# Moving operands of two feed-forward stages placed at many different addresses modulo 256 bytes

## The chip, the cores and the metric

One core of one Trainium2 chip runs the kernel. The metric is device microseconds from one launch, lower is better; times are given as the median of several runs. A profile is one execution of the program taken by the hardware profiler; its times are counted from its first instruction to its last (the span).

## What is computed

One decoder layer for a sequence of 512 tokens with a model width of 1024, in float32. Two feed-forward blocks (FFN 1 and FFN 2, inner width 2816) stand around a mixer that has two attention branches. Only the FFNs are touched by the change:

```python
def swiglu_ffn(x, g, w_gate, w_up, w_down):
    h = rms_norm(x, g)
    return (jax.nn.silu(h @ w_gate) * (h @ w_up)) @ w_down

x = x + 0.5 * swiglu_ffn(x, ffn1_norm, ffn1_w_gate, ffn1_w_up, ffn1_w_down)
# RMS norm, one wide projection, forgetting attention (branch A),
# top-k sparse attention (branch B), gated merge, output projection
x = x + merged @ w_out
x = x + 0.5 * swiglu_ffn(x, ffn2_norm, ffn2_w_gate, ffn2_w_up, ffn2_w_down)
```

## The kernel before

**Precision.** TensorE is fed in fp32r. Every float32 operand is split into a high and a low part, and each product takes three matmuls: high by high, low moving by high weights, high moving by low weights (`mm3`, L129 to L132). A name that ends in `h` or `l` is the high or the low part. In `PE.matmul(out, a, b)` the first operand is the stationary one (the weights, loaded by a LDWEIGHTS of 128 columns ahead of each matmul) and the second is the moving one, which is streamed past it.

**Orientation.** In the FFNs the weights are stationary (`wh`, `wl`, three buffers each of 128x1024) and the activations move: their features lie on the 128 partitions and the 512 tokens along a partition.

**Stages of an FFN** (`ffn`, L182). The 22 blocks of 128 inner features are worked in three groups: blocks 0 to 7, 8 to 15, 16 to 21.

- Blocks 0 to 5 are done plainly: eight k-steps of `mm3` with 512 moving columns for the gate product (`pg`) and again for the up product (`pu`), with `xh`, `xl` moving.
- The other sixteen blocks are done in eight pairs of blocks (`pair_steps`, L307) by a scheme that needs seven half-size products in place of eight. `product` (L317) runs 24 matmuls of 256 moving columns each, so that a pair takes 7 x 24 = 168 of them, and the two FFNs 2 x 8 x 168 = 2688. What moves here are combinations of the normalized input, made once by `combine` (L235) on VectorE and ScalarE: `b1` (once a pair), `tb`, `ta`, `b2` (twice a pair), each a high and a low tile made by `parts_tile` (L219) in the pool `halves`. They write to the PSUM tiles `pA`, `pB`, `pC`.
- After each group, `run_down` (L396) multiplies by the down weights: `pd`, 512 moving columns, where the group's activations move. Two blocks share one tile. The tiles `a0h` to `a2l` (made in `act_tiles`, L190, one set for all three groups) hold the first six blocks of a group; the last two blocks of the first and the second group lie in stream buffers (`ax`). In the last step of FFN 2 the 512 columns are done as twice 256, so that 36 matmuls there have 256 columns.

Of the 1038 matmuls of `pd` with 512 columns, 846 have one of `a0h` to `a2l` moving and 192 have `ax`. The profile shows `a0h`, `a1h`, `a2h` as `ah` and the low ones as `al`.

**Places.** A tile's address along its partition is set by the pools: tiles stand one behind another, and all sizes around are such that nearly every one begins at 96 modulo 256 bytes. In the built program this holds for all weights of the FFNs (`wh`, `wl`, and each 128-column slice of them, since slices are 512 bytes apart), for `xh`, `xl`, `ax`, for `a0h` to `a2l`, and in the mixer for `mh`, `ml` (moving in `ps_out`) and for the weights `wh`, `wl` that move in `ps_t` against `xh`, `xl`. The exception is the pool `halves`: a tile of 8 floats named `pad` (L188) stands ahead of it, so that `b1`, `tb`, `ta`, `b2` begin at 128 modulo 256. Steps within a tile are 1024 or 2048 bytes, so that each matmul of a tile begins at the tile's place. Below, *place* means the first byte of the moving operand modulo 256.

**Order.** TensorE's order of work is written out by hand (steps in `ffn`, weights loaded and split up to three steps ahead); the scheduler orders the other engines. The low part of the activations of most blocks (L204, L205) is made with a DMA that adds onto the negated high part, issued from GpSimd's queue.

Of the kernel before, what the change touches and what calls it, by code (L numbers as in the profile page):

```python
# [11 lines left out]
F32 = mybir.dt.float32  # L12
F32R = mybir.dt.float32r
# [5 lines left out]
P = 128  # L19
T = 512  # L20
# [22 lines left out]

GROUPS = ((0, 8), (8, 16), (16, 22))
PLAIN = 6
HT = T // 2
HK = KD // 2

# [2 lines left out]
def tile_hybrid_layer(ctx: ExitStack, tc: tile.TileContext, a: dict):  # L51
# [14 lines left out]
    def tmp_tile(name):  # L66
        return tmp.tile([P, T], F32, tag="t", name=name)
# [28 lines left out]
    def stream(i, dtype, name):  # L96

        return xpool.tile([P, 2 * T], dtype, tag=f"X{i}", name=name)
# [83 lines left out]
    def ffn(n, nxt, parts=lambda d: [slice(0, T)]):  # L182
        wg, wu, wp, wd = (a[f"w_{nm}{n}"] for nm in ("gate", "up", "pair", "down"))
        gi = 0 if n == 1 else 2
        with tc.tile_pool(name=f"ffn{n}", bufs=1) as ap, tc.tile_pool(name=f"halves{n}", bufs=1) as hp:
            act = {}

            hp.tile([P, 8], F32, name="pad")  # L188

            def act_tiles(f):  # L190

                q, lo = f // 2, next(lo for lo, hi in GROUPS if lo <= f < hi)
                j = q - lo // 2
                if q not in act:
                    act[q] = ([ap.tile([P, 2 * T], F32R, tag=f"a{j}{i}", name=f"a{i}") for i in "hl"]
                              if j < 3 else [stream(6 + i, F32R, "ax") for i in range(2)])
                return [t[:, f % 2 * T:f % 2 * T + T] for t in act[q]]

            def split_act(f, u, late):

                h, l = act_tiles(f)
                S.copy(h, u)  # L202
                if late:
                    S.mul(l, h.bitcast(F32), -1.0)  # L204
                    G.dma_start(l, u, accum_op=OP.add)  # L205
                else:
                    V.tensor_sub(l, u, h.bitcast(F32))  # L207

            def activate(f, pg, pu, rb):
# [5 lines left out]
                V.tensor_mul(u, u, g)  # L215
                split_act(f, u, 1 < f < PLAIN)


            def parts_tile(nm, cols):  # L219
                return [hp.tile([P, HK * cols], F32R, tag=nm + i, name=nm + i)  # L220
                        .rearrange("p (k t) -> p k t", k=HK) for i in "hl"]

            ops = {}

            def operand(nm, cols=T):
                if nm not in ops:
                    ops[nm] = parts_tile(nm, cols)
                return ops[nm]

            def split_to(nm, k, src, cols=T):  # L230
                h, l = (t[:, k] for t in operand(nm, cols))
                S.copy(h, src)
                V.tensor_sub(l, src, h.bitcast(F32))

            def combine(k):  # L235
# [3 lines left out]
                for dst, d in ((lo, k), (hi, k + HK)):  # L239
                    V.scalar_tensor_tensor(dst, x[d], gains[:, gi, d:d + 1], rbs[0], op0=OP.mult, op1=OP.mult)  # L240
                split_to("b1", k, lo[:, :HT], HT)
                yield
                ta, tb = tmp_tile("ta"), tmp_tile("tb")
                V.tensor_sub(ta[:, :HT], lo[:, :HT], lo[:, HT:])
                V.scalar_tensor_tensor(tb[:, :HT], ta[:, :HT], -1.0, hi[:, HT:], op0=OP.mult, op1=OP.subtract)
                V.tensor_sub(ta[:, HT:], hi[:, HT:], lo[:, HT:])
                V.scalar_tensor_tensor(tb[:, HT:], tb[:, :HT], -1.0, hi[:, :HT], op0=OP.mult, op1=OP.subtract)
                split_to("tb", k, tb)
# [5 lines left out]
            def moving(nm, half):  # L254
                h, l = ops[nm]
                sl = slice(half * HT, half * HT + HT)
                return (h, l) if nm == "b1" else (h[:, :, sl], l[:, :, sl])
# [17 lines left out]
            def plain(src, f, run):  # L275
                raw = {}

                def split():
                    return [t[:, :f * P].rearrange("p (n m) -> p n m", n=f) for t in split_w(raw["a"][0], f * P)]
                return Step(raw, [("a", f, src)], split, run, "a")  # L280
# [3 lines left out]
            def run_gate(f):  # L284
                def run(w):
                    pg[0] = fm_product(w, "pg", mid if f == 1 and n == 2 else {})
                    if f == 1 and n == 2:
                        activate(0, *pair0, held[0])
                        rbs.append(held[0])
                return run  # L290

            def run_up(f):
                def run(w):
                    if f == 1 and n == 1:

                        pu = fm_product(w, "pu", mid, psum.tile([P, T], F32, tag="s", bufs=2, name="pu1"))
                        activate(0, *pair0, held[0])
                        rbs.append(held[0])
                    else:
                        pu = fm_product(w, "pu")  # L300
                    if f == 0:
                        pair0.extend((pg[0], pu))
                    else:
                        activate(f, pg[0], pu, rbs[0])
                return run

            def pair_steps(q, last):  # L307
# [78 lines left out]

                load = {z: (z, 0, wp[q - PLAIN // 2, i]) for i, z in enumerate("abcd")}
                return [Step(raw, [load["c"], load["d"], load["a"]], split_a, run_a),
# [7 lines left out]
            def run_down(d, lo, hi):  # L396
                def run(w):
                    order = [k for k in range(hi - lo - 2)] + [hi - lo - 1, hi - lo - 2]
                    end = hi == KF

                    for cols in parts(d) if end else [slice(0, T)]:
                        ps = acc_tile("pd")[:, cols]
                        for k in order:
                            h, l = act_tiles(lo + k)
                            mm3(ps, w[0][:, k], w[1][:, k], h[:, cols], l[:, cols], k == order[0], k == order[-1])
                        V.scalar_tensor_tensor(x[d][:, cols], ps, 0.5, x[d][:, cols], op0=OP.mult, op1=OP.add)  # L406
                        if end:
                            nxt(d, cols)
                return run
# [3 lines left out]
            for lo, hi in GROUPS:  # L413
                for f in range(lo, min(hi, PLAIN)):
                    if f or not first:
                        steps += [plain(wg[f], KD, run_gate(f)), plain(wu[f], KD, run_up(f))]
                for q in range(max(lo, PLAIN) // 2, hi // 2):
                    steps += pair_steps(q, 2 * q + 2 == hi)
# [70 lines left out]
    gq = const.tile([P, 2], F32, name="gq")  # L489
    V.tensor_scalar(gq, hg[:, 0:2], -0.125, None, op0=OP.mult)  # L490
    ffn(1, lambda d, cols: (prep(d, 1), add_square(d)))


    with tc.tile_pool(name="mix", bufs=1) as mp, ExitStack() as att_ctx:
        at = att_ctx.enter_context(tc.tile_pool(name="att", bufs=1))
# [293 lines left out]
        for h in range(H):  # L789
# [3 lines left out]
            for i in range(1, NT):  # L793
                n = P * (i + 1)
# [156 lines left out]
        for g in range(2 * H):  # L951
            lo_eng[0] = G if g < 2 else V
            q, k, bias = nq, nk, nb
# [59 lines left out]


    ffn(2, lambda d, cols: nc.sync.dma_start(a["y"][:, d, cols], x[d][:, cols]),
        lambda d: [slice(0, T)] if d < KD - 1 else [slice(0, T // 2), slice(T // 2, T)])


def _fm(w):

    k, n = w.shape
    return w.reshape(k // P, P, n // P, P).transpose(2, 1, 0, 3)
# [22 lines left out]
def _layout(x, ffn1_norm, ffn1_w_gate, ffn1_w_up, ffn1_w_down, mix_norm, w_in, b_forget,  # L1045
# [7 lines left out]
    for n, (g, u, dn) in ((1, (ffn1_w_gate, ffn1_w_up, ffn1_w_down)), (2, (ffn2_w_gate, ffn2_w_up, ffn2_w_down))):  # L1053
        o[f"w_gate{n}"] = _fm(g)[:PLAIN]
        o[f"w_up{n}"] = _fm(u)[:PLAIN]

# [37 lines left out]
```

## Time and profile before

| | |
|---|---|
| three runs, median (lowest to highest) | 1114.56 us (1112.28 to 1116.45) |
| span of the profiled execution | 1111.9 us |
| TensorE matmul busy | 1084.2 us, 98% of the span, 6664 matmuls |
| TensorE weight load busy | 967.0 us, 87% |
| VectorE, ScalarE, GpSimd busy | 769.8, 539.5, 218.5 us |
| granted TensorE clock, mean | 0.994 |

The profiled execution's own device time is not listed beside its span; the median of the runs is 2.7 us above the span and the lowest run 0.4 us above it. A matmul's own duration in the profile (0.28 us for 256 columns) is longer than the distance to the next one's start, since matmuls overlap in the pipeline. What a matmul costs is therefore read from the distance between starts: the length of a stretch in which nothing waits, divided by the number of matmuls that begin in it.

### The profile page before, as it was taken

What the parts mean: (1) busy time and instruction counts of PE and PEld (TensorE: products, weight loads), DVE (VectorE), ACT (ScalarE), POOL (GpSimd) and SP (SyncE); (2) the same over time, 40 slices, a digit from 0 to 9 for tenths busy, and PEclk for the clock granted to TensorE, in tenths of its full rate; (3) what the DMA queues carried; (4) which work ended last, traced back from release to release, by engine and by line L of the source; (5) the groups of instructions that cost most, each with busy time, mean ns of one, the idle gap of its engine ahead of it and who ended that gap; (6) DMA issues with size and microseconds to landing.
All of it is one profiled execution on the core that took longest, in us unless ns stands there. A gap on an engine that the chain in (4) does not pass through costs nothing.

```text
span 1111.9 us, 17413 instructions
## 1 busy us (share of the span) xinstructions
PE 1084.2 (98%) x6664; PEld 967.0 (87%) x6664; DVE 769.8 (69%) x1228; ACT 539.5 (49%) x862; POOL 218.5 (20%) x263
## 2 busy tenths in 40 slices
PE   8999999999999997899999999999999999999998
PEld 6788899989988897899778778888889899989997
DVE  5995578746966599966664666764976478755963
ACT  5653155513644653467655676443544245522551
POOL 0000000000002347677842561000000000000000
PEclk9999999999999999899999999999999999999999
DMA  7334235532442224335324411433245325432441
GB/s 244 107 98 146 88 97 151 139 100 84 110 115 92 76 76 118 110 112 151 101 76 143 122 59 38 126 121 97 93 124 143 94 77 153 135 97 91 124 115 67
DMA packets 43236, 122.61 MB, mean 110 GB/s; under 512 B 5641, under 2 KB 6025, under 8 KB 43153
## 3 DMA queue, kind: packets, MB, share of 16 engines
q1 hardware_dynamic: 38976, 113.89, 33.7%
q0 software_dynamic: 4032, 7.34, 3.9%
q8 instruction: 53, 0.87, 0.3%
q10 hardware_dynamic: 144, 0.26, 0.1%
q14 instruction: 31, 0.25, 0.1%
HBM read 103.63 MB, written 2.11 MB: 95 GB/s over the span
## 4 chain that ended last, share of the span: by engine, by line
PE 81%; DVE 8%; ACT 4%; POOL 3%; issue 3%; DMA 2%; SPq 0%; POOLq 0%; DVEq 0%; ACTq 0%
PE pd L131 7%; PE pd L132 7%; PE pd L130 7%; PE pB L132 4%; PE pB L131 4%; PE pB L130 4%; PE pC L132 3%; PE pA L132 3%; PE pA L131 3%; PE pC L131 3%; PE pA L130 3%; PE pC L130 3%; PE ps_f L130 2%; PE ps_f L131 2%; PE ps_f L132 2%
## 5 line engine op out<-in xcount | busy, mean ns | idle before, releaser
L131 PE MATMUL pd<-al,wh 128*128 128x512 f32 (+1 forms) x294 | 113.4, 386 | 0.5 <-DVE al L207 0.5
L130 PE MATMUL pd<-ah,wh 128*128 128x512 f32 (+1 forms) x294 | 113.4, 386 | 0.2
L132 PE MATMUL pd<-ah,wl 128*128 128x512 f32 (+1 forms) x294 | 113.1, 385 | 0.0
L205 POOL DMA_DIRECT2D al<-gu x20 | 17.1, 855 | 428.9 <-ACT al L204 428.9
L112 ACT CAST wh<-s 128x1024 fp32r<-128x1024 f32 x48 | 50.6, 1055 | 93.9 <-PE pB L131 39.3
L406 DVE SCALAR_TENSOR_TENSOR x<-pd,x 128x512 f32<-128x512 f32 (+1 forms) x49 | 33.3, 680 | 88.6 <-PE pd L132 88.4
L130 PE MATMUL ps_t<-wh,xh 128*128 128x256 f32 (+1 forms) x288 | 83.2, 289 | 0.0
L131 PE MATMUL ps_t<-wl,xh 128*128 128x256 f32 (+1 forms) x288 | 82.7, 287 | 0.0
L132 PE MATMUL ps_t<-wh,xl 128*128 128x256 f32 (+1 forms) x288 | 82.6, 287 | 0.0
L130 PE MATMUL pB<-tbh,wh 128*128 128x256 f32 x256 | 71.4, 279 | 0.0
L131 PE MATMUL pB<-tbl,wh 128*128 128x256 f32 x256 | 71.4, 279 | 0.0
L132 PE MATMUL pB<-tbh,wl 128*128 128x256 f32 x256 | 71.4, 279 | 0.0
L130 PEld LDWEIGHTS pd<-ah,wh 128*128 128x128 f32 x294 | 55.2, 188 | 11.9 <-ACT ah L202 1.0
L131 PEld LDWEIGHTS pd<-al,wh 128*128 128x128 f32 x294 | 55.2, 188 | 11.8 <-DVE al L207 1.1
L132 PEld LDWEIGHTS pd<-ah,wl 128*128 128x128 f32 x294 | 55.2, 188 | 11.0
L113 DVE TENSOR_TENSOR wl<-s,wh 128x1024 fp32r<-128x1024 f32 x48 | 58.5, 1219 | 3.8 <-ACT wh L112 3.8
L131 PEld LDWEIGHTS ps_t<-wl,xh 128*128 128x128 f32 x288 | 56.7, 197 | 0.5
L130 PEld LDWEIGHTS ps_t<-wh,xh 128*128 128x128 f32 x288 | 56.8, 197 | 0.4
L132 PEld LDWEIGHTS ps_t<-wh,xl 128*128 128x128 f32 x288 | 56.7, 197 | 0.0
L112 ACT CAST wh<-re 128x1024 fp32r<-128x1024 f32 (+1 forms) x27 | 27.8, 1028 | 57.4 <-PE pd L131 22.2
L112 ACT CAST wh<-ra 128x1024 fp32r<-128x1024 f32 (+1 forms) x29 | 29.8, 1029 | 51.6 <-PE pd L131 23.4
L819 ACT ACTIVATE p<-p,mn 128x512 f32<-128x512 f32 (+1 forms) x64 | 35.9, 561 | 37.0 <-DVE mn L817 36.8
(326 smaller groups left out, 3604.9 us busy)
## 6 DMA issues: line engine op xcount, KB each, us to landing
rc<-in_w_pair_dram SPq DMA_DIRECT2D x13, 512.0 KB, 3.6
re<-in_w_pair_dram SPq DMA_DIRECT2D x13, 512.0 KB, 3.6
ra<-in_w_pair_dram SPq DMA_DIRECT2D x13, 512.0 KB, 3.5
rd<-in_w_pair_dram SPq DMA_DIRECT2D x13, 512.0 KB, 3.6
rb<-in_w_pair_dram SPq DMA_DIRECT2D x12, 512.0 KB, 3.7
al<-gu POOLq DMA_DIRECT2D x20, 256.0 KB, 4.1
ra<-in_w_down_dram SPq DMA_DIRECT2D x7, 512.0 KB, 3.5
rc<-in_w_down_dram SPq DMA_DIRECT2D x7, 512.0 KB, 3.6
```

The source lines that it names most:

```text
L112: S.copy(wh[:, :f], raw[:, :f])
L113: V.tensor_sub(wl[:, :f], raw[:, :f], wh[:, :f].bitcast(F32))
L130: PE.matmul(out, lh, rh, start=start, stop=False, **more)
L131: PE.matmul(out, lh, rl, start=False, stop=False, **more)
L132: PE.matmul(out, ll, rh, start=False, stop=stop, **more)
L205: G.dma_start(l, u, accum_op=OP.add)
L406: V.scalar_tensor_tensor(x[d][:, cols], ps, 0.5, x[d][:, cols], op0=OP.mult, op1=OP.add)
L819: S.activation(p, p, AF.Exp, bias=mn, scale=-1.0, accum_out=rs)
```

## The change

`SHIFTS` lists a number of bytes for each tile of moving operands, 14 for each FFN. `shifted` makes the tile 64 floats (256 bytes) wider, and the operand is the slice that begins that many bytes into it. The numbers are handed out in the order in which the tiles are first asked for. `act_tiles` and `parts_tile` take their tiles from it, and the tile `pad` goes. The weights' buffers, `xh`, `xl`, `ax` and all of the mixer are where they were.

```diff
+SHIFTS = {1: (16, 48, 64, 80, 96, 112, 128, 144, 16, 32, 48, 64, 80, 96),
+          2: (160, 176, 192, 208, 224, 240, 8, 40, 112, 128, 160, 192, 224, 240)}
...
-            hp.tile([P, 8], F32, name="pad")
+            shift = iter(SHIFTS[n])
+            place_at = {}
+
+            def shifted(pool, cols, tag):
+
+                if tag not in place_at:
+                    place_at[tag] = next(shift)
+                at = place_at[tag] // 4
+                return pool.tile([P, cols + 64], F32R, tag=tag, name=tag)[:, at:at + cols]
...
-                    act[q] = ([ap.tile([P, 2 * T], F32R, tag=f"a{j}{i}", name=f"a{i}") for i in "hl"]
+                    act[q] = ([shifted(ap, 2 * T, f"a{j}{i}") for i in "hl"]
...
-                return [hp.tile([P, HK * cols], F32R, tag=nm + i, name=nm + i)
-                        .rearrange("p (k t) -> p k t", k=HK) for i in "hl"]
+                return [shifted(hp, HK * cols, nm + i).rearrange("p (k t) -> p k t", k=HK) for i in "hl"]
```

In the built program no instruction is added, removed or moved: each engine has the same instructions in the same order, and names apart they read the same. Only addresses differ. The places that follow, with the number of matmuls in which the tile moves (before, all tiles of the first half of the table were at 128 and all of the second half at 96):

| tile | FFN 1: place, matmuls | FFN 2: place, matmuls |
|---|---|---|
| b1h, b1l (256 columns) | 160, 128; 176, 64 | 32, 128; 48, 64 |
| tbh, tbl | 192, 256; 208, 128 | 64, 256; 80, 128 |
| tah, tal | 224, 256; 240, 128 | 104, 256; 136, 128 |
| b2h, b2l | 112, 256; 128, 128 | 208, 256; 224, 128 |
| a0h, a0l (512 columns) | 112, 96; 144, 48 | 0, 100; 16, 50 |
| a1h, a1l | 144, 96; 160, 48 | 0, 100; 32, 50 |
| a2h, a2l | 176, 96; 192, 48 | 64, 100; 80, 50 |

Of the counts of FFN 2 in the last three rows, 8 (high) and 4 (low) each are the matmuls with 256 columns.

## Prediction

> **What bounds the kernel now.** I read the page's summary first.
>
> ```profile
> span 1111.9 us, 17413 instructions
> PE 1084.2 (98%) x6664; PEld 967.0 (87%) x6664; DVE 769.8 (69%) x1228; ACT 539.5 (49%) x862; POOL 218.5 (20%) x263
> PE 81%; DVE 8%; ACT 4%; POOL 3%; issue 3%; DMA 2%; SPq 0%; POOLq 0%; DVEq 0%; ACTq 0%
> ```
>
> TensorE is busy for 98% of the span, and the last line, the chain of waits that ended last, is TensorE for 81%. No instruction moves in this change, so the question is only what one matmul costs, and whether anything that now hides behind TensorE comes out. For the first I looked at the table of windows over stretches in which nothing waits. Its columns are the stretch, the sum, TensorE's busy time and the number of matmuls that touch it, the granted clock, and DMA.
>
> ```profile
> 139.64:218.04 78.40, 78.40 (x673) 1.00 0.47 129
> 720.13:763.65 43.52, 43.52 (x194) 1.00 0.39 126
> 354.14:364.85 10.71, 10.71 (x98) 1.00 0.33 112
> 403.14:421.85 18.71, 18.71 (x158) 1.00 0.18 57
> ```
>
> The windows run from the start of a stretch's first matmul to the start of the first one behind it, and the count takes in a neighbour or two that overlap an edge. What they hold is read from the timeline at their edges:
>
> ```profile
> 139.64 0.28 PE L130 MATMUL pA<-b1h,wh 128*128 128x256 f32 x1
> ...
> 217.93 0.28 PE L132 MATMUL pC<-b2h,wl 128*128 128x256 f32 x1
> 218.04 0.39 PE L130 MATMUL pd<-ah,wh 128*128 128x512 f32 x1
> ...
> 354.14 0.26 PE L130 MATMUL ps_t<-wh,xh 128*128 128x208 f32 x1
> ...
> 403.14 0.28 PE L130 MATMUL ps_t<-wh,xh 128*128 128x256 f32 x1
> ...
> 720.13 0.39 PE L130 MATMUL ps_out<-mh,wh 128*128 128x512 f32 x1
> ...
> 1104.13 0.28 PE L130 MATMUL pd<-ah,wh 128*128 128x256 f32 x1
> ...
> 1108.32 0.28 PE L132 MATMUL pd<-ah,wl 128*128 128x256 f32 x1
> ```
>
> The distances between starts that follow:
>
> - Pair stage, four pairs of FFN 1, 672 matmuls of 256 columns at place 128: 78.40 / 672 = 116.67 ns.
> - `ps_t`, 156 matmuls of 256 columns whose moving operand is at place 96: 18.71 / 156 = 119.94 ns.
> - Last step of FFN 2, 36 matmuls of 256 columns at place 96: (1108.32 - 1104.13) / 35 = 119.7 ns. The weights are the same buffers as in the pair stage, and their place is 96 in all three.
> - `ps_out`, 192 matmuls of 512 columns at place 96: 43.52 / 192 = 226.67 ns.
> - `ps_t`, 96 matmuls of 208 columns: 10.71 / 96 = 111.6 ns.
>
> So the place does cost something. The same form, 256 columns against weights at 96, takes 3.3 ns more from place 96 than from place 128 (119.94 - 116.67). And 512 columns take 226.67 - 119.94 = 106.7 ns more than 256 at place 96, which is then the streaming of 256 columns. Taken off, an overhead of 13.2 ns a matmul is left at place 96, for either length, and of 9.9 ns at place 128. These are the only two places of which the trace has long clean stretches. The change leaves 96 in all of its acts and keeps 128 for a single tile of halves, so nearly all of its places have no row.
>
> **The change, part by part.**
>
> The number of matmuls, from the groups by form:
>
> ```profile
> L131 PE MATMUL pd<-al,wh 128*128 128x512 f32 x282 | 110.0, 390 | 0.5 <-DVE al L207 0.5
> L130 PE MATMUL pB<-tbh,wh 128*128 128x256 f32 x256 | 71.4, 279 | 0.0
> L130 PE MATMUL pA<-b1h,wh 128*128 128x256 f32 x128 | 35.7, 279 | 0.0
> ```
>
> The halves: `tb` in `pB` has 3 x 256, and `b1` in `pA`, `b2` in `pA` and `pC`, `ta` in `pB` and `pC` have 3 x 128 each, 768 + 5 x 384 = 2688 matmuls, 313.6 us at 116.67 ns. The acts: 3 x 282 = 846 of 512 columns, 191.8 us at 226.67 ns, and the 36 of 256 columns. TensorE is never late in these stages, so a nanosecond more for each is 2.7 us for the halves and 0.9 us for the acts, all of it on the end.
>
> *Halves.* They leave 128, the cheaper of the two places known. From above, 119.94 ns bounds a place that is as dear as 96: 2688 x 3.27 = +8.8 us if all were so. From below, the 208-column stretch bounds what a matmul with its own weight load can come to: 111.6 ns, where 208 columns of streaming (208/256 x 106.7 = 86.7 ns) no longer set it, so -5.1 x 2688 = -13.7 us. Between these ends I take the rows that have the same form: a place draws 116.67 or 119.94 with equal weight, 118.3 ns in the mean, +1.64 x 2688 = +4.4 us.
>
> *Acts.* They leave 96, the dearer of the two. By the same draw 512 columns take 226.67 or 226.67 - 3.27 = 223.4 ns, in the mean -1.64 x 882 = -1.4 us. All at the cheap price is -2.9 us; none cheaper is 0. Upwards, the mixer has rows of 512 columns at place 96 shortly after a stall:
>
> ```profile
> 366.23 0.40 PE L132 MATMUL ps_f<-xh,wl 128*128 128x512 f32 x1
> 366.46 0.40 PE L130 MATMUL ps_f<-xh,wh 128*128 128x512 f32 x1
> 366.70 0.39 PE L131 MATMUL ps_f<-xl,wh 128*128 128x512 f32 x1
> ...
> 367.85 0.39 PE L130 MATMUL ps_f<-xh,wh 128*128 128x512 f32 x1
> ```
>
> Seven distances in 1.62 us are 231 ns each; later in the run they settle at 226.67. If the high and low parts, now at different places in turn, kept the stream from settling, that is +4.8 x 846 = +4.1 us. What speaks against: at the switch from halves (128) to acts (96), 217.93 to 218.04 above and the 0.23 us to the next, no such distances show.
>
> *Two halves at an odd 8 bytes.* `tah` and `tal` of FFN 2 begin at 104 and 136, which no other operand here does; 384 matmuls. No row has this. Doubling the streaming would be 384 x 106.7 ns = 41 us, no loss is 0; I take 0, as the nearest rows (places a multiple of 32) differ by 3 ns only, and leave the rest to a small chance. [...]
>
> *Writers.* ScalarE, VectorE and the adding DMA write these tiles, and some of the places are not a multiple of 32. The profile of `al`:
>
> ```profile
> L205 POOL DMA_DIRECT2D al<-gu x20: 841/858/862, 161.9 to 1061.0; - x20
> L207 DVE TENSOR_TENSOR al<-gu,ah x4: 683/687/693, 321.4 to 1078.3; 128x512 fp32r<-128x512 f32 x4
>   PE pd L131: 0.5, 2
> DMA to landing us min/median/max: 3.3/4.1/6.4
> ```
>
> TensorE waits 0.5 us in all for these tiles, on VectorE twice. A pair takes 168 x 0.1167 = 19.6 us, and a landing that came 1 us later has that room for all pairs but a group's last, whose low part VectorE makes (the x4 above). I cost this at nothing; if a write were 10% longer the last pairs would show it as 4 x 0.07 = 0.3 us.
>
> *Sum.* +4.4 - 1.4 = +3.0 us. The profiled span of 1111.9 us would become 1114.9; the median of the runs is 2.7 us above the span, and 1114.56 + 3.0 = 1117.5 us.
>
> **Rivals.**
>
> 1. *Slower: the price is that of a boundary, and place 128 stood on it.* If a stream costs 3.27 ns more whenever it begins off a multiple of 128 bytes (96 is off, 128 on), only `b2l` of FFN 1 keeps the cheap price among the halves: 2560 x 3.27 = +8.4 us; `a0h` and `a1h` of FFN 2 at place 0 gain 200 x 3.27 = 0.7 us. That is +7.7, 1122.3 us. With a boundary of 64 bytes 640 halves (places 64, 128, 192) stay and 348 acts (0, 64, 192) gain: +6.7 - 1.1 = +5.6, 1120.1 us. For it: both known prices fit, and lengths are multiples of 1024, so only the start can matter. It decides above the average if more than 2 of 3 halves are dear: with the acts at -1.4, 5.6 us needs 2140 of 2688. Against: two points do not make a boundary.
>
> 2. *No loss: what costs is sharing the weights' place.* At 96 the moving operand and the weights that load meanwhile begin at the same byte modulo 256. If this alone costs 3.27 ns, the halves stay at 116.67 ns and the acts and the last step win: -3.27 x 882 = -2.9 us, 1111.7 us. For it: it fits the two places as well. [...] No row here separates the two readings.
>
> 3. *Faster: 128 is not the best place.* An overhead of 9.9 ns is left there, and the 208-column stretch shows 111.6 ns as reachable. If the mean place lies halfway down to it, halves gain 2.55 x 2688 = 6.9 us and the acts, down from 13.2 to 7.4 ns of overhead, 5.8 x 882 = 5.1: 1102.6 us. For it: the two places known differ by a quarter of the overhead. Against: neither has less than 9.9. [...]
>
> 4. *Worse than any known place.* The alternation of places or the two at an odd 8 bytes make streams dearer than at 96: halves at 120 ns and acts at 231, +8.8 + 4.1 = +12.9, 1127.5 us.
>
> **How the numbers follow.** A measurement of this kernel tells about 0.5%, 5.6 us, from no change. The forecast (+3.0) has 0.40, of which 0.06 lies above +5.6 since the draw is made for 16 tiles of halves of unequal weight. Rival 1 has 0.29, nearly all slower (0.26; 0.03 for the 64-byte form just below). Rival 2 has 0.13, no change. Rival 3 has 0.12, faster. Rival 4 has 0.06, slower. Faster 0.12; same 0.34 + 0.03 + 0.13 = 0.50; slower 0.06 + 0.26 + 0.06 = 0.38. The range leaves out the better half of rival 3 and most of rival 4: 1106 to 1124 us.
>
> **What would show it.** In the profile after, the pair stages of both FFNs as windows by product: each product has one pair of places, so a product of 24 matmuls reads 2.80 us at 116.67 ns and 2.88 at 119.94. The forecast has both kinds. Rival 1 has 2.88 nearly everywhere but in products with `tb` (if 64 bytes count); rival 2 has 2.80 everywhere and `pd` at 223.4 ns; rival 3 has products below 2.75 us. Rival 4 shows in `ta` of FFN 2, or in `pd` above 227. The mixer's windows must read as before. The prediction is wrong in its ground if products of one place differ with the tile, or if TensorE's waits for `ah` or `al` grow past a microsecond.

## The result and the profile after

The changed kernel takes 1123.48 us (median of 4 runs, 1120.98 to 1125.59), the kernel before in the same rounds 1113.79 us. The ratio is 1.0084, with a 95% interval of 1.0060 to 1.0107: slower by 9.7 us. The profiled execution of it ran 1125.12 us, 1.7 us above its span.

The page's summary of the kernel after:

```profile
span 1123.4 us, 17413 instructions
PE 1096.0 (98%) x6664; PEld 973.6 (87%) x6664; DVE 770.9 (69%) x1228; ACT 539.3 (48%) x862; POOL 217.0 (19%) x263
```

TensorE is busy 11.8 us longer (1096.0 against 1084.2) with the same 6664 matmuls; VectorE and ScalarE are where they were, within 1.1 us. So the loss is in what a matmul costs. The table of windows over the kernel after shows where; the first two are the first stretch of `pd` (192 matmuls, 48 of them with `ax`) and the pair stretch behind it (672 matmuls) in FFN 1, the next two the same in FFN 2, the fifth `ps_out`.

```profile
96.30:140.76 44.46, 44.46 (x195) 1.00 0.32 95
140.76:220.06 79.30, 79.30 (x673) 1.00 0.47 127
856.33:901.03 44.70, 44.70 (x195) 1.00 0.32 95
901.03:980.94 79.91, 79.91 (x674) 1.00 0.45 126
726.12:769.64 43.52, 43.52 (x194) 1.00 0.39 126
```

The same stretches of the kernel before, as far as they weren't shown:

```profile
95.90:139.64 43.74, 43.74 (x194) 1.00 0.31 96
849.97:893.71 43.74, 43.74 (x195) 1.00 0.32 97
893.71:972.11 78.40, 78.40 (x673) 1.00 0.47 128
```

Busy equals the window in the FFN rows, so nothing waited; the matmuls stand further apart. Halves: 79.30 / 672 = 118.0 ns in FFN 1 and 79.91 / 672 = 118.9 in FFN 2, against 116.67. Over 1344 matmuls each that is +1.8 and +3.0 us. `pd`: 44.46 / 192 = 231.6 ns and 44.70 / 192 = 232.8, against 43.74 / 192 = 227.8. Over the 528 and 510 matmuls of 512 columns that is +2.0 and +2.5 us. Together that is +9.3 us of the measured 9.7. `ps_out`, whose operands didn't move, still takes 226.67 ns. The stretch between the FFNs, with the plain steps of FFN 2, takes 478.30 us here and 476.23 in the profile before, with the same work; in the kernel with the acts alone moved (below) it takes 473.67, so this difference comes and goes without the change.

The acts' rows in the timeline of the kernel after, near the start of that `pd` stretch of FFN 2, show the new distances one by one: three matmuls in 0.71 us, where three at 226.67 ns take 0.68.

```profile
857.26 0.40 PE L135 MATMUL pd<-a0l,wh 128*128 128x512 f32 x1
857.50 0.39 PE L136 MATMUL pd<-a0h,wl 128*128 128x512 f32 x1
857.73 0.40 PE L134 MATMUL pd<-a1h,wh 128*128 128x512 f32 x1
857.97 0.40 PE L135 MATMUL pd<-a1l,wh 128*128 128x512 f32 x1
```

A product of `b2` in FFN 2, high at 208 and low at 224, shows it for the halves: its 24 matmuls take 120 ns each.

```profile
912.42:915.30 2.88, 2.88 (x26) 1.00 0.12 21
```

### The profile page after: what moved, and what is told of

It reads as the page before. It is cut to its first block, busy times and chain, and to the rows that moved or that the text cites. A ratio compares the mean times of both kernels' runs of the same rounds, so it can differ in the third digit from the quotient of the medians.

```text
span 1123.4 us, 17413 instructions
## 1 busy us (share of the span) xinstructions
PE 1096.0 (98%) x6664; PEld 973.6 (87%) x6664; DVE 770.9 (69%) x1228; ACT 539.3 (48%) x862; POOL 217.0 (19%) x263
## 4 chain that ended last, share of the span: by engine, by line
PE 78%; DVE 8%; ACT 4%; POOL 3%; issue 3%; DMA 2%; SPq 0%; POOLq 0%; DVEq 0%; ACTq 0%
PE pd L135 7%; PE pd L136 7%; PE pd L134 7%; PE pB L135 4%; PE pB L136 4%; PE pB L134 4%; PE pA L135 3%; PE pC L135 3%; PE pC L134 3%; PE pC L136 3%; PE pA L134 3%; PE pA L136 3%; PE ps_f L134 2%; PE ps_f L135 2%; PE ps_f L136 2%
## 5 line engine op out<-in xcount | busy, mean ns | idle before, releaser
L217 POOL DMA_DIRECT2D a0l<-gu x8 | 6.8, 854 | 327.2 <-ACT a0l L216 327.2
L116 ACT CAST wh<-rc 128x1024 fp32r<-128x1024 f32 (+1 forms) x28 | 28.8, 1028 | 50.9 <-PE pd L135 20.6
L134 PE MATMUL ps_f<-xh,wh 128*128 128x512 f32 x128 | 51.4, 402 | 0.0
L135 PE MATMUL ps_f<-xl,wh 128*128 128x512 f32 x128 | 50.8, 397 | 0.0
L116 ACT CAST wh<-rb 128x1024 fp32r<-128x1024 f32 (+1 forms) x28 | 28.5, 1020 | 46.2 <-PE pd L135 21.4
L136 PE MATMUL ps_f<-xh,wl 128*128 128x512 f32 x128 | 50.7, 396 | 0.0
L832 POOL TENSOR_SCALAR p<-p,rs 128x512 f32<-128x512 f32 (+1 forms) x64 | 37.4, 587 | 62.1 <-DVE rs L831 50.1
```

The costliest lines, as they stand in the source:

```text
L116: S.copy(wh[:, :f], raw[:, :f])
L134: PE.matmul(out, lh, rh, start=start, stop=False, **more)
L135: PE.matmul(out, lh, rl, start=False, stop=False, **more)
L136: PE.matmul(out, ll, rh, start=False, stop=stop, **more)
L832: G.tensor_scalar(p, p, rs, 1.0, op0=OP.mult, op1=OP.mult)
```

## The experiments

Three theories stood. *Place*: each place of the moving operand has a price of its own (the prediction's rival 1 is one form). *Distance*: the price hangs on the moving place minus the weights' place (rival 2 is one form). *Alternation*: neighbours at different places keep the stream from settling (rival 4). All edits below are to the changed kernel; numbers in `SHIFTS` are distances to the weights' place 96, modulo 256, handed out in the order a0, b1, tb, ta, b2, a1, a2, each high then low. Where a list is the same for many tiles it is written short here.

### The two parts apart

```diff
+SHIFTS = {1: (0, 0, 64, 80, 96, 112, 128, 144, 16, 32, 0, 0, 0, 0),
+          2: (0, 0, 192, 208, 224, 240, 8, 40, 112, 128, 0, 0, 0, 0)}      # halves only
...
+SHIFTS = {1: (16, 48, 32, 32, 32, 32, 32, 32, 32, 32, 48, 64, 80, 96),
+          2: (160, 176, 32, 32, 32, 32, 32, 32, 32, 32, 160, 192, 224, 240)}      # acts only
```

> The change's halves alone; acts back at 96 (distance 0). The sums of distances in the profile of the change: halves +4.9 us, acts +4.2, ax +0.5. If the two parts add: +4.9 us over before, acts and ax at 226.7 ns again. By the prediction's draw: +4.4.

> The change's acts alone; halves all at 128 as before. If the parts add: +4.7 us over before (acts +4.2, ax +0.5), halves at 116.67 ns. By the prediction's draw: -1.4 us.

Halves alone: ratio 1.0051 (1.0033 to 1.0069), acts alone 1.0034 (1.0020 to 1.0048), which is 5.7 and 3.8 us of 1114.09. The sum, 0.85%, agrees with the whole change's 0.84%; each part agrees with its expectation (+4.9 and +4.7) within its interval. Windows of the kernel with halves alone (`pd`, pairs of FFN 1, pairs of FFN 2):

```profile
96.54:140.28 43.74, 43.74 (x195) 1.00 0.32 96
140.28:219.56 79.28, 79.28 (x673) 1.00 0.45 127
895.07:974.98 79.91, 79.91 (x673) 1.00 0.46 126
```

And with acts alone (`pd`, pairs of FFN 1):

```profile
96.23:140.73 44.50, 44.50 (x195) 1.00 0.30 95
140.73:219.13 78.40, 78.40 (x673) 1.00 0.48 129
```

Each part's stretches read as in the full change (79.28 and 79.91; 44.50) and the other part's as before (43.74; 78.40). The prediction's -1.4 us for the acts is out.

### One place for all, and two in turn

```diff
+SHIFTS = {1: (32,) * 14, 2: (32,) * 14}          # all at 128
...
+SHIFTS = {1: (64,) * 14, 2: (160,) * 14}         # 160 in FFN 1, 0 in FFN 2
...
+SHIFTS = {1: (32, 0) * 7, 2: (0, 32) * 7}        # high and low in turn
```

> All 28 tiles at place 128, so halves as before the change and acts moved from 96 to 128, one place for all. Alternation theory (a matmul is dear when its neighbours' moving operands begin at other places; one place for all settles): halves 116.7 ns, acts between 223.4 and 226.7 ns without spread, ax at 226.7 again; 1111 to 1114 us. Place theory (each place has a price of its own, whatever the neighbours): the same halves, acts 223.4 ns, 1111 us. If acts stay near 231 ns, the wider tiles themselves are at fault and both fall.

> One place in each FFN: 160 in FFN 1, 0 in FFN 2, for halves and acts. Alternation theory: both FFNs settle, halves at one distance between 113 and 120 ns and acts at one between 223 and 227, time 1109 to 1119 us. Place theory with a boundary of 128 bytes (rival 1): FFN 1 halves 119.9 and acts 226.7, FFN 2 halves 116.7 and acts 223.4, 1117 us. Weights' place theory (rival 2: only sharing place 96 with the weights costs): 116.7 and 223.4 in both FFNs, 1111 us.

> Only the two places known from before, in turn: high parts at 128 and low parts at 96 in FFN 1, the reverse in FFN 2. Alternation theory: halves at 118.5 ns or more in both FFNs, acts at 230 or more, +8 us or more over before. Place theory: prices add, FFN 1 halves (2 x 116.67 + 119.94) / 3 = 117.8 ns, FFN 2 halves 118.9, acts 224.5 and 225.6, +3 us, and two distances, one for each place.

All at 128: ratio 1.0039 (1.0024 to 1.0054). Its windows (`pd`, pairs):

```profile
95.42:140.15 44.73, 44.73 (x194) 1.00 0.30 94
140.15:218.56 78.41, 78.41 (x674) 1.00 0.46 129
```

The halves are back at 116.7 ns, but the acts, all at one place, take 44.73 / 192 = 233.0 ns: the very shift of 32 bytes that makes 256 columns cheaper makes 512 columns dearer, by more. The acts pay this without any alternation, and the extrapolation from 256 columns to 512 was wrong. The expectation's last sentence laid such a result to the wider tiles; that doesn't hold either, since in the run with halves alone the acts lie in the same wider tiles at distance 0 and take 43.74 us.

160 and 0: ratio 1.0068 (1.0053 to 1.0083). FFN 1, then FFN 2:

```profile
96.67:141.02 44.35, 44.35 (x195) 1.00 0.31 95
141.02:220.16 79.14, 79.14 (x673) 1.00 0.46 127
850.68:895.48 44.80, 44.80 (x195) 1.00 0.31 94
895.48:975.22 79.74, 79.74 (x673) 1.00 0.45 126
```

Halves at 160 take 117.8 ns and at 0 take 118.7; acts 231.0 and 233.3. Place 0, a multiple of 256, isn't the cheap one that a boundary of 128 bytes asks for, and neither place comes to the 116.7 and 223.4 of rival 2.

High and low in turn: ratio 1.0062 (1.0043 to 1.0081). FFN 1, then FFN 2:

```profile
95.94:140.45 44.51, 44.51 (x194) 1.00 0.30 95
140.45:219.61 79.16, 79.16 (x673) 1.00 0.47 127
856.76:901.27 44.51, 44.51 (x195) 1.00 0.31 95
901.27:979.92 78.65, 78.65 (x674) 1.00 0.47 128
```

Halves: 117.8 ns in FFN 1, where adding the two prices gives 117.8; 117.0 in FFN 2, where it gives 118.9. Acts: 231.8 ns in both, where 233.0 and 227.8 add to 231.3 and 229.5. Prices of neighbours don't simply add, in either direction, but between these two places no stretch is dearer than at the dearer place. The time, 6.9 us over before, lies between the two expectations of +3 and +8: the place theory had the acts at 128 too cheap (223.4 ns), alternation the halves too dear.

That doesn't clear alternation for every pair of places. In the changed kernel itself `b2` of FFN 2 has its high part at distance 112 and its low part at 128. The map below has 113.4 and 119.3 ns for these, and 115.4 if they add; its products take 119.6 to 120.0 ns in every pair, as if all were at the dearer distance. So two distances in turn can cost more than they add up to, and the map, made with high and low alike, doesn't tell how much.

### The weights moved instead

```diff
     wpool = ctx.enter_context(tc.tile_pool(name="wpool", bufs=3))
+    wpool.tile([P, 8], F32, name="wpad", bufs=1)     # wh, wl from 96 to 128
     tmp = ctx.enter_context(tc.tile_pool(name="tmp", bufs=6))
+    tmp.tile([P, 56], F32, name="tpad", bufs=1)      # all behind stays in place
+SHIFTS = {n: (32,) * 2 + (64,) * 8 + (32,) * 4 for n in (1, 2)}     # acts 128, halves 160
```

> Weights and FFN operands all moved on by 32 bytes: weights at 128, halves at 160, acts at 128; distances between moving operand and weights as before the change. Weights' distance theory: halves 116.7 ns and acts 226.7 as before; xh, ax and mh at 96 against weights at 128 get a new distance and may change. Place theory with boundary (price by the moving operand's own address): halves 119.9 at place 160, acts 223.4 at place 128, xh, ax, mh at 226.7 as before, about +5.9 us.

Ratio 1.0078 (1.0058 to 1.0098). Windows: the long run of 156 `ps_t`, then `pd`, pairs, `ps_out`.

```profile
405.61:423.82 18.21, 18.21 (x157) 1.00 0.18 58
97.49:141.67 44.18, 44.18 (x195) 1.00 0.31 95
141.67:220.07 78.40, 78.40 (x674) 1.00 0.47 129
724.19:768.99 44.80, 44.80 (x193) 1.00 0.37 121
```

This run decides between place and distance. Halves at place 160 against weights at 96 took 117.8 ns (above); at 160 against weights at 128 they take 78.40 / 672 = 116.67, as 128 against 96. And `ps_out`, of which nothing moved but its weights' buffers, goes from 43.52 to 44.80 us, 226.67 to 233.33 ns. So the price follows the distance between the moving operand and the weights, not the place of the moving operand alone. In `ps_t`, where `wh` and `wl` move against `xh` and `xl` at 96, the same shift makes the distance 32, and its 256 columns go from 119.9 to 18.21 / 156 = 116.7 ns, as the halves have it there. The loss of this kernel is put down to everything that moves from 96 (`xh`, `xl`, `ax`, `mh`, `ml`) against weights at 128, at distance -32, which is 224: by the windows +1.28 us in `ps_out` and +0.44 in the `pd` stretch with its `ax`. The `pd` row holds 48 matmuls of `ax` as well; the acts among it, at distance 0, are at 227.8 by their start times.

### Only the low weights moved

```diff
     tmp = ctx.enter_context(tc.tile_pool(name="tmp", bufs=6))
+    tmp.tile([P, 56], F32, name="tpad", bufs=1)      # all behind stays in place
+    wpad = []
...
         wh = wpool.tile([P, 1024], F32R, tag="wh", name="wh")
+        if not wpad:
+            wpad.append(wpool.tile([P, 8], F32, name="wpad", bufs=1))   # wl alone to 128
         wl = wpool.tile([P, 1024], F32R, tag="wl", name="wl")
+SHIFTS = {n: (0,) * 2 + (32,) * 8 + (0,) * 4 for n in (1, 2)}     # as before the change
```

> Only the buffers of the low weights (wl) moved on by 32 bytes, to 128; wh at 96, halves at 128, acts at 96 as before the change. Matmuls run high by wh, low by wh, high by wl. If the price comes from the load that runs meanwhile (the next matmul's weights), the low-by-wh matmul, under which wl loads, changes alone: halves 120 ns against 116.7 for the others, acts 233 against 226.7. If it comes from a matmul's own weights, the high-by-wl matmul changes alone by the same. If distances do not add one by one, all three change.

A single execution: 1128.3 us beside 1114.8. `pd`, pairs, `ps_out`, and then nine matmuls of `ps_out` in the timeline:

```profile
97.97:142.82 44.85, 44.85 (x194) 1.00 0.32 94
142.82:221.97 79.15, 79.15 (x674) 1.00 0.46 127
727.46:772.25 44.79, 44.79 (x193) 1.00 0.38 121
```

```profile
740.05 0.40 PE L138 MATMUL ps_out<-mh,wh 128*128 128x512 f32 x1
740.29 0.40 PE L139 MATMUL ps_out<-ml,wh 128*128 128x512 f32 x1
740.53 0.39 PE L140 MATMUL ps_out<-mh,wl 128*128 128x512 f32 x1
...
742.15 0.40 PE L138 MATMUL ps_out<-mh,wh 128*128 128x512 f32 x1
```

Nine matmuls take 2.10 us, 233.3 ns each, as if all the weights had moved, though a third of them did. By the start times to the nanosecond, the mean distance from a matmul's start to the next is 232.0 ns for high by `wh`, 239.2 for low by `wh` (under which `wl` loads) and 228.8 for high by `wl`; all were 226 to 227. The largest change is where the moved buffer loads, which speaks for the load that runs meanwhile; but all three change, so that neither simple reading holds alone, and the run is inconclusive on that point.

### A map of distances

```diff
+SHIFTS = {1: (16, 16, 16, 16, 48, 48, 80, 80, 96, 96, 16, 16, 16, 16),
+          2: (96, 96, 112, 112, 128, 128, 144, 144, 176, 176, 96, 96, 96, 96)}
...
+SHIFTS = {1: (128, 128, 192, 192, 208, 208, 224, 224, 240, 240, 128, 128, 128, 128),
+          2: (240, 240, 8, 8, 24, 24, 40, 40, 32, 32, 240, 240, 240, 240)}
```

> A map of distances (moving place minus weights' place 96, modulo 256), high and low at one place: halves b1 16, tb 48, ta 80, b2 96 in FFN 1 and 112, 128, 144, 176 in FFN 2; acts 16 in FFN 1, 96 in FFN 2. Distance theory: each product shows a distance between starts of its own, the same in every pair, between 113 and 121 ns for halves; acts settle nowhere but at 0, 229 to 235 ns. Alternation theory: 24 matmuls at one place settle, so every product ends at 116.7 to 120 and acts at 226.7 or less. Time 1116 to 1121 us by the first, 1112 to 1115 by the second.

> The rest of the map: halves at distances 192, 208, 224, 240 in FFN 1 and 8, 24, 40, 32 in FFN 2; acts 128 in FFN 1, 240 in FFN 2. Distance theory: b2 of FFN 2 (distance 32) is 116.7 ns as before, the others between 113 and 121; acts 229 to 235. If odd 8 bytes cost by themselves, the products at 8, 24, 40 stand apart from their neighbours in the map by more than 3 ns; by the distance theory they do not.

Single executions: 1126.3 and 1124.7 us beside 1114.8. High and low have the same distance. A product is 24 matmuls. From the first kernel, `b1` at distance 16 in the first, second and third pair of a group and `b1` at 112, then `pd` with acts at 16 and 96:

```profile
140.55:143.40 2.85, 2.85 (x25) 1.00 0.00 0
160.50:163.23 2.73, 2.73 (x27) 1.00 0.09 30
180.42:183.21 2.79, 2.79 (x26) 1.00 0.04 15
...
902.60:905.37 2.77, 2.77 (x26) 1.00 0.00 0
...
96.03:140.55 44.52, 44.52 (x194) 1.00 0.32 95
857.80:902.60 44.80, 44.80 (x195) 1.00 0.32 94
```

From the second, products at distances 8, 24 and 32, then `pd` with acts at 240:

```profile
899.96:902.84 2.88, 2.88 (x26) 1.00 0.00 0
849.69:852.59 2.90, 2.90 (x26) 1.00 0.06 21
852.59:855.40 2.81, 2.81 (x26) 1.00 0.59 187
855.40:899.96 44.56, 44.56 (x195) 1.00 0.31 95
```

The means over all products, with the distances of the other runs, in ns (for 512 columns a `pd` stretch with its `ax` in it, as above):

| distance | 0 | 8 | 16 | 24 | 32 | 40 | 48 | 64 | 80 | 96 |
|---|---|---|---|---|---|---|---|---|---|---|
| 256 columns | 119.9 | 120.0 | 116.7 | 120.6 | 116.7 | 120.0 | 118.3 | 117.8 | 119.2 | 119.9 |
| 512 columns | 227.8 | | 231.9 | | 233.0 | | | 231.0 | | 233.3 |

| distance | 112 | 128 | 144 | 160 | 176 | 192 | 208 | 224 | 240 |
|---|---|---|---|---|---|---|---|---|---|
| 256 columns | 113.4 | 119.3 | 118.7 | 118.7 | 119.2 | 117.8 | 118.7 | 118.2 | 117.3 |
| 512 columns | 231.8 | 232.4 | | 233.3 | 231.9 | | | | 232.1 |

(112 for 256 columns is from the next run; `b1` in the map has 114.5.) The ranges that the distance theory expected are met for both lengths, and 24 matmuls at one place don't settle to the known prices, as alternation asks. Two things expected of it are not met. The time of the first kernel was to be 1116 to 1121 us and is 1126.3. And a product isn't always the same in every pair: `b1` at distance 16 takes 118.8 ns in the first pair of each group, 113.7 in the second and 116.5 in those behind, as the rows show, with the same moving tiles at the same places; `ta` at 80 takes 118.3 to 120.0 and `tb` at 208 takes 116.7 to 119.3. So a distance doesn't fix the price alone; something that changes from pair to pair, not found here, counts too, and the table's entries are means over such products. For 512 columns distance 0, where the acts stood, is the best of ten; for 256 columns distance 32, where the halves stood, is among the best, and one beats it. The odd 8 bytes: 8, 24 and 40 all read 120.0 to 120.6, while their neighbours 16 and 32 read 116.7. That is more than 3 ns, so by the expectation's own measure the odd 8 bytes cost something by themselves. But 0 and 96, multiples of 16, read 119.9 as well, so these runs don't settle it.

### The best distance for the halves

```diff
+SHIFTS = {n: (0,) * 2 + (112,) * 8 + (0,) * 4 for n in (1, 2)}     # halves at place 208
```

> All halves at place 208, distance 112, the one of the map with the cheapest product (b1 in FFN 2, 114.5 ns); acts at distance 0 as before. If the price goes with the distance: halves 114.5 ns, -2.15 x 2688 = -5.8 us, 1107 to 1109 us, faster than both kernels. If the 114.5 belonged to that product's neighbours or tile: between 116.7 and 120, no gain or a loss.

1106.28 us against 1114.09, ratio 0.9937 (0.9918 to 0.9955): faster than both kernels. `pd`, pairs of FFN 1, pairs of FFN 2:

```profile
95.77:139.56 43.79, 43.79 (x195) 1.00 0.31 96
139.56:215.75 76.19, 76.19 (x673) 1.00 0.47 132
889.59:966.61 77.02, 76.48 (x673) 1.00 0.48 131
```

76.19 / 672 = 113.4 ns, 3.3 less than before: 2688 x 3.3 = 8.8 us of gain in the matmuls; measured are 7.0 us (0.63%), with an interval of 5.0 to 9.1. The product's lower price was not its neighbours' or its tile's: all halves have it now, 113.3 to 113.9 ns by tile where nothing waits. In FFN 2 TensorE idles for once, 77.02 against 76.48 busy. The waits of that window name the step that is late next:

```profile
PE pB L134 <- DVE u L380: 0.5, 1, 0.5
```

### The same in the mixer, and for 512 columns

```diff
+    def parts_w(at=0):
+        return [wpool.tile([P, 1088], F32R, tag=nm, name=nm)[:, at:at + 1024] for nm in ("wh", "wl")]
...
-                    c[3] = load_w(*c[:3])
+                    c[3] = load_w(*c[:3], at=28 if c[2] == 256 else 0)     # ps_t: w moves at 208
+SHIFTS = {n: (0,) * 2 + (112,) * 8 + (0,) * 4 for n in (1, 2)}
...
+SHIFTS = {1: (112,) * 14, 2: (176,) * 2 + (112,) * 8 + (176,) * 4}     # the other kernel
```

> Halves at distance 112 in both FFNs and, in the mixer, the 768 matmuls ps_t of 256 columns moved from distance 0 to 112 (w's buffers 256 bytes wider, the moving slice 112 bytes on; xh, the weights there, stay at 96). Distance theory: ps_t falls from 119.6 to 113.4 ns, up to -4.8 us more than the halves alone (-7 us), less what the attention's own waits give back; 1102 to 1105 us. If the gain belonged to the FFNs' tiles: ps_t unchanged, 1106 us.

> Halves at distance 112; acts (512 columns) at 112 in FFN 1 and 176 in FFN 2, high and low alike, two distances not yet tried for this length. Distance theory with a price for each length: no bound known; the rows so far put 512 columns at 229 to 235 ns at every distance but 0, so about +4 us against halves at 112 alone. If a distance that suits 256 columns suits 512: acts at 220 to 226 ns, faster by up to 5 us.

With `ps_t` at 112 as well: 1105.06 us against 1112.87, ratio 0.9923 (0.9901 to 0.9945); the interval overlaps that of the halves alone, so the runs don't tell the two apart. In the profile they differ. The long run of 156 `ps_t`:

```profile
399.40:417.13 17.73, 17.73 (x157) 1.00 0.19 60
```

17.73 / 156 = 113.7 ns against 119.9: the price comes with the distance to another pair of tiles in another stage, with the roles of weights and activations exchanged. (The places are again 208 against 96, so this row doesn't tell distance from place; the run with the weights moved does.)

Acts at 112 and 176: a single execution, 1109.37 us, 3 us above the median of the kernel with the halves alone at 112; `pd` takes 44.50 and 44.52 us, 231.8 and 231.9 ns. The distance that is best for 256 columns costs 512 columns 4 ns.

```profile
95.97:140.47 44.50, 44.50 (x194) 1.00 0.32 95
846.83:891.35 44.52, 44.52 (x194) 1.00 0.32 95
```

## Why the prediction was right or wrong

The time lay within the range, 1123.5 us near its upper end of 1124, but the sum behind it did not hold: it gave +3.0 us, and +9.7 came. The likeliest case, no change that can be told, did not come; slower, at 0.38, did, and most of that chance stood on rival 1, which falls. So the time came within the range by the range's width and with luck, not by the mechanism. Step by step:

- *TensorE alone sets these stages, and writers stay hidden.* Right. Busy and window agree in every FFN stretch, and TensorE's wait for the low acts is 0.5 us in all, as before.
- *A place has a price, read from 128 against 96.* Right as a reading of these two; what the price hangs on was left open between rivals 1 and 2, and is the distance to the weights (the run with the weights moved). It isn't one price for each: at one distance the same moving tiles took 113.7 to 118.8 ns, and two distances in turn don't add.
- *Halves +4.4 us.* The size is right, +4.8 by the windows, but with luck. The draw between two known prices gave a mean of 118.3 ns; the kernel has 118.0 and 118.9, and the mean over the 19 distances of the map is 118.4, which two rows couldn't tell: distances take values from 113.4 to 120.6. Nor is it the sum of the distances' own prices: with the map's means, high counted twice, that is +3.2 us. The largest part that is missing is `b2` of FFN 2, 119.8 ns where 115.4 adds up.
- *Acts -1.4 us.* Wrong, in sign. The step that failed is "by the same draw 512 columns take 226.67 or 223.4": it carried the 3.3 ns from 256 columns to 512. At distance 32 the 512 columns cost 5.2 ns more in the `pd` stretch (233.0 against 227.8), not 3.3 less, and no distance tried is better than 0, where they stood. What it rested on, that 512 columns take 106.7 ns more than 256 for their streaming and the rest is an overhead of the place for either length, was the author's estimate from two rows at distance 0 (226.67 and 119.94 ns), and no run shows the split: at 32 the lengths differ by 233.0 - 116.7 = 116.3 ns. The part's own upper bound, +4.1 us from the `ps_f` rows behind a stall, was the size, for a cause that isn't needed: +4.5 measured, `ax` included. What was held against that bound, the switch from halves to acts, shows nothing, since both neighbours there stand at distances that suit them, 116.7 ns at 32 and 227.8 at 0 (argued, not tried).
- *Odd 8 bytes at no cost.* Nearly: `ta` of FFN 2 takes 120.0 ns. Over the mean distance's 118.4 that is 384 x 1.6 = 0.6 us, and over the 116.7 of the neighbours 16 and 32 it is 1.3 us.
- *Rival 1* (a boundary of 128 or 64 bytes) falls: place 0 costs 118.7 ns for halves and 233.3 for acts, and halves at 160 cost 117.8 or 116.67, as the weights stand. (Its 2140 of 2688 is four halves of five, not two of three.)
- *Rival 2* had the cause, distance, and the wrong price for the acts: sharing the weights' place is among the dearest for 256 columns, 119.9 ns, and the best of the ten distances for 512 columns, 227.8 ns. That the weights' place counts shows in `ps_out`, which goes from 226.67 to 233.33 ns when its weights alone are moved by 32 bytes.
- *Rival 3*: not what the change does, since its mean place is dearer; but a place with less than 9.9 ns of overhead was found, if the prediction's own estimate is kept: at distance 112, 113.4 - 106.7 leaves 6.7 ns. Its row of 111.6 ns isn't one of a single place: the 208-column slices of `wh` begin 832 bytes apart, at distances 0, 64, 128 and 192 in turn.
- *Rival 4* named the right size for the acts (231 ns) for a reason that isn't needed: acts all at one place cost as much. Its signs came, `pd` above 227 ns and `ta` of FFN 2 at 120.0, and for `b2` of FFN 2 two distances in turn do cost more than they add up to.

What stays open is the mechanism. No run here shows why 112 suits 256 columns and 0 suits 512, how the three loads of a triple act on one another, or why one distance gives different prices in different pairs.

## What to carry to other kernels

When a stream of matmuls with a weight load each is the bound, measure the distance between starts in clean stretches, and take the addresses of moving operand and weights, modulo 256 as this change sets them, as something to tune: it was worth 0.6 to 0.8% here. A price found for one length did not carry to another; 32 bytes took 3.3 ns off 256 columns (119.94 to 116.67) and put 5.2 ns onto 512 (227.8 to 233.0). A map is cheap: one place per product gave eight distances in one profile, and its best entry, 114.5 ns in one product, held when all 2688 matmuls were put there, at 113.3 to 113.9 ns by tile where nothing waits. It holds for high and low at one distance; a mixture has to be measured for itself, as `b2` of FFN 2 with 119.8 ns where 115.4 adds up.

## What the runs showed of the hardware that was not expected

- The time between matmul starts in this kernel went with the moving operand's address minus the weights' address, taken modulo 256 as the change sets it: in the mean 256 columns from 113.4 to 120.6 ns over 19 distances, 512 columns from 227.8 to 233.3 over ten, with a granted clock of 1.00 in the windows shown.
- A step of eight bytes changed the time of 256 columns: distances 24, 32 and 40 took 120.6, 116.7 and 120.0 ns, the first and the last in a single execution.
- The same moving tiles at the same distance, 16, took 113.7, 116.5 or 118.8 ns a matmul, by the pair's position in its group (a single execution).
- Moving only the low weights' buffers, a third of the loads, cost 512 columns as much as moving all of them: 44.79 and 44.80 us for `ps_out` against 43.52 before, the first from a single execution.
- Matmuls whose own places didn't move changed with their neighbours': `ax`, at distance 0, stood at 230 to 233 ns by its start times in most runs that have the acts elsewhere (231.7 and 232.6 in the two FFNs of the changed kernel), and at 227 when they were at 0 too. With acts at 240 it stayed at 227, so not every neighbour did it.
